# Differential attention inside a transformer block: accumulators copied out of PSUM, squares on VectorE, the causal mask as a matmul

## The chip, the cores and the metric

One Trainium2 chip, all 8 NeuronCores. Each core computes one element of a batch of 8, with no exchange between cores. The metric is the time of the slowest core in microseconds (us), from its first to its last instruction. Most executions of a kernel agree to 0.3%. Some fall into a slower state, in which cores of one die, or of both, show a lower granted TensorE clock (0.83 in place of 0.95 in the 5348.14 us execution of run 1 below); those runs are marked slow and are left out of every comparison.

## The reference, cut to what matters

A block of a hybrid encoder for 2048 frames of width 2048: one RMS norm and input projection, two mixers side by side (differential attention and an mLSTM), a gated merge, an MLP, a gated embedding, a last norm. Only the attention is touched here. It has 8 heads, each with two softmax maps of 64 channels over one value of 128:

```python
s = einsum('bqhmd,bkhmd->bhmqk', q * 64**-0.5, k)     # m = 2 maps per head
mask = (key // 64) <= (query // 64)                   # chunks of 64 frames
a = softmax(where(mask, s, NEG_INF))
w = a[:, :, 0] - lam * a[:, :, 1]
o = rmsnorm(einsum('bhqk,bhkd->bqhd', w, v), sub_g)   # over the 128 channels of a head
```

## The kernel before

Attention runs in units. A unit is a query tile of 256 rows (`qt`) against a pair of key blocks (`jp`); a head has 36 units, and tile `qt` has `qt + 1` of them, the last being the diagonal one. Scores go to PSUM banks 0 to 3 (two units in flight), the exponentials to SBUF, and the products with the values accumulate in banks 4 and 5. A 129th column of ones makes the softmax sum. Between the units, a filler issues matmuls of other jobs (the next head's K and Q, a V job, gates, the mLSTM's convolution) into banks 6 and 7. The program issues a list to each engine. ScalarE and VectorE work through theirs in order.

```python
def attn(h):
    for u in range(36 * h, 36 * h + 36):
        _, qt, jp = UN[u]
        B.act(E[u % 3], <scores of u>, AF.Exp, scale=0.125)          # ScalarE
        if jp == qt:                                                 # the causal mask
            B.memset("dve", e_[64:128, :, 0, 0:64], 0.0)
            B.memset("dve", e_[64:128, :, 1, 128:192], 0.0)
        s_mm(u + 1)                                                  # TensorE: next scores
        yield                                                        # TensorE: 3 to 4 filler matmuls
        av_mm(u)                                                     # TensorE: exponentials x values
        tick()                                                       # work that was put off
        if jp == qt:
            finalize(h, qt)
            # ... cut: after tiles 3 and 7, ya_norm two units later, ya_out six units later

def finalize(h, qt):
    for i in range(2):                                               # two blocks of 128 rows
        acc, r_ = <bank 4 + i>, rsb[b % 4]
        # VectorE: reciprocal of the two sums, r2 = r1 * -lambda   (cut)
        B.ts("dve", o_head[:, b, :], acc[:, 0, 0:128], r_[:, 0:1], ALU.mult)
        B.stt("dve", o_head[:, b, :], acc[:, 1, 0:128], r_[:, 2:3], o_head[:, b, :], ALU.mult, ALU.add)
        B.act(sqj, o_head[:, b, :], AF.Square, accum=ssa[h % 2][:, b:b + 1])   # ScalarE
```

The softmax here doesn't subtract the row's maximum and nothing guards it: scores larger than these inputs give would overflow.

Of the kernel before, what the change touches and what calls it, by code (L numbers as in the profile page):

```python
# [7 lines left out]
F32 = mybir.dt.float32  # L8
BF16 = mybir.dt.bfloat16
U8 = mybir.dt.uint8  # L10
AF = mybir.ActivationFunctionType
ALU = mybir.AluOpType
# [226 lines left out]
def build():  # L239
    B = Builder()  # L240
# [29 lines left out]
    R = lambda off, shape, dt: cv(O_R + off, shape, dt)  # L270
# [3 lines left out]
    def small(shape, dt=F32):  # L274
        n = 1
        for s_ in shape[1:]:
            n *= s_
        nb = al(n * DTS[dt])
        o = sm[0]
        sm[0] += nb  # L280
        assert sm[0] <= O_SM + SM_BYTES, sm[0]
        return cv(o, shape, dt)
# [22 lines left out]
    ssa = [small([128, 16]) for _ in range(2)]  # L305
# [3 lines left out]
    psum = es.enter_context(nc.psum_tensor("ps", [128, 4096], F32))  # L309

    def bank(i):
        return psum[:, 512 * i:512 * (i + 1)]
# [31 lines left out]
    for t_, v_, cmp_, pat, cm in ((ident_b, 0.0, ALU.not_equal, -1, 1), (ident_f, 0.0, ALU.not_equal, -1, 1),  # L344
# [3 lines left out]
            out=t_, in_=t_, pattern=[[pat, 128]], compare_op=cmp_, fill=1.0 - v_, base=0, channel_multiplier=cm),  # L348
# [77 lines left out]
    o_head = R(24704, [128, 16, 128], F32)  # L426
    ya_tok = [R(32896 + 2048 * i, [128, 8, 128], BF16) for i in range(2)]
    yast = [R(36992 + 2048 * i, [128, 1024], BF16) for i in range(2)]
    E = [R(76288 + 2048 * i, [128, 2, 2, 256], BF16) for i in range(3)]
    sqj = R(82432, [128, 128], BF16)  # L430

    xst = [R(41088 + 8192 * i, [128, 4, 512], F32) for i in range(7)]
    nsq = [R(24704 + 2048 * i, [128, 512], F32) for i in range(3)]
# [63 lines left out]
    for t in range(4):  # L497
# [7 lines left out]
        n = 0  # L505
        for _ in work():
            n += 1
            if n < 80:
                if n % 4 == 0:
                    if next(gen, None) == "ones":  # L510
                        n = 80
# [7 lines left out]
    B.memset("pool", Vb[1][:, :, :, 128:129], 1.0)  # L519


    pend = []
    side = [iter(())]

    def tick():
        next(side[0], None)
        for it in list(pend):
            it[0] -= 1
            if it[0] <= 0:
                pend.remove(it)  # L530
                it[1]()

    def attn_units():
        return [(h, qt, jp) for h in range(8) for qt in range(8) for jp in range(qt + 1)]

    UN = attn_units()

    def s_mm(u):
        h, qt, jp = UN[u]
        kv, qv = KQ[h % 2][:, 0, :], KQ[h % 2][:, 1, :]  # L540
        sb = 2 * (u % 2)
        for jj in range(2):
            j = 2 * jp + jj
            for m in range(2):
                B.mm(bank(sb + m)[:, jj * 256:(jj + 1) * 256], kv[64 * m:64 * m + 64, j * 128:(j + 1) * 128],
                     qv[64 * m:64 * m + 64, qt * 256:(qt + 1) * 256], True, True)

    def av_mm(u):
        h, qt, jp = UN[u]
        e_ = E[u % 3]  # L550
        vv = Vb[h // 4]
        last = jp == qt
        for i in range(2):
            for jj in range(2):
                if last and jj > i:
                    continue
                j = 2 * jp + jj
                for m in range(2):
                    B.mm(bank(4 + i)[:, m * 256:m * 256 + 129], e_[:, m, jj, i * 128:(i + 1) * 128], vv[:, j, h % 4, :],
                         j == 0 and m == 0, last and jj == i and m == 1, skip=True)  # L560

    def finalize(h, qt):
        for i in range(2):
            b = 2 * qt + i
            acc = bank(4 + i).rearrange("p (m d) -> p m d", m=2, d=256)
            r_ = rsb[b % 4]
            B.op("dve", lambda e, acc=acc, r_=r_: e.reciprocal(out=r_[:, 0:2], in_=acc[:, :, 128]), [acc[:, :, 128]], [r_[:, 0:2]])  # L567
            B.tt("dve", r_[:, 2:3], r_[:, 1:2], neglam, ALU.mult)
            B.ts("dve", o_head[:, b, :], acc[:, 0, 0:128], r_[:, 0:1], ALU.mult)
            B.stt("dve", o_head[:, b, :], acc[:, 1, 0:128], r_[:, 2:3], o_head[:, b, :], ALU.mult, ALU.add)  # L570
            B.act(sqj, o_head[:, b, :], AF.Square, accum=ssa[h % 2][:, b:b + 1])

    def ya_norm(h, hf):
        s8 = slice(8 * hf, 8 * hf + 8)
        ss, rs = ssa[h % 2][:, s8], rsa[h % 2][:, s8]
        B.ts("pool", rs, ss, 1.0 / 128.0, ALU.mult, EPS, ALU.add)
        B.tt("pool", rs, rs, nhalf[:, 0:8], ALU.pow)
        for b in range(8):
            B.ts("dve", ya_tok[hf][:, b, :], o_head[:, 8 * hf + b, :], rs[:, b:b + 1], ALU.mult)

    def ya_out(h, hf):
        bk = fb.get()
        for b in range(8):
            B.tp(bank_bf(bk)[:, b * 128:(b + 1) * 128], ya_tok[hf][:, b, :], ident_b)
        B.act(yast[hf], bank_bf(bk), AF.Copy, scale=subg)
        B.dma("sp", f"ya{hf}", scr_ya[h * 2 + hf], yast[hf])

    def attn(h):
        u0 = 36 * h
        for u in range(u0, u0 + 36):  # L590
            _, qt, jp = UN[u]
            if u == 0:
                s_mm(0)
            e_ = E[u % 3]
            sb = 2 * (u % 2)
            B.act(e_.rearrange("p m j q -> p (m j q)"), psum[:, 512 * sb:512 * sb + 1024], AF.Exp, scale=0.125)
            if jp == qt:
                B.memset("dve", e_[64:128, :, 0, 0:64], 0.0)
                B.memset("dve", e_[64:128, :, 1, 128:192], 0.0)
            if u + 1 < len(UN) and UN[u + 1][0] == h:  # L600
                s_mm(u + 1)
            yield
            if u + 1 < len(UN) and UN[u + 1][0] != h:
                s_mm(u + 1)
            av_mm(u)
            tick()
            if jp == qt:
                finalize(h, qt)
                if qt in (3, 7):
                    pend.append([2, lambda h=h, hf=qt // 4: ya_norm(h, hf)])  # L610
                    pend.append([6, lambda h=h, hf=qt // 4: ya_out(h, hf)])
# [264 lines left out]
    for h in range(8):  # L876
        nf = 0
        nextq = None
        if h < 7:
            nextq = kq_job(h + 1)  # L880
            fill.add(nextq)
            nf += 128
        if h == 2:
            fill.add(v_job(1))
            nf += 64
        if h == 3:
            nf += 192
        if h == 4:
            fill.add(gates())
            nf += 40  # L890
        if h == 7:
            fill.add(mqk_job(0, 0))
            nf += 128
        drive(attn(h), 36, nf)
        if h == 3:
            fill.drain()
        elif h < 7:
            fill.drain(nextq)
# [57 lines left out]
    def tmp():  # L956
        cnt["t"] += 1
        return tmps[cnt["t"] % 6]
# [44 lines left out]
    for hf in range(2):  # L1003
# [10 lines left out]
        for np_ in range(8):  # L1014
            k, w = wget(f"wo{np_}")
            for nn in range(2):
                n = 2 * np_ + nn
# [8 lines left out]
                while lagged:  # L1026
                    a_ = lagged.pop(0)
# [6 lines left out]
        for qd in range(4):  # L1034
            for np_ in range(8):
                k, w = wget(f"up{qd}_{np_}")
                for nn in range(2):
                    n = 2 * np_ + nn
                    for tt in range(2):
                        bk = mm_chain(lambda kc: w[:, kc, nn * 128:(nn + 1) * 128], lambda kc: h2[:, kc, tsl[tt]], 16)  # L1040
                        r_ = tmp()
# [9 lines left out]
            for np_ in range(8):  # L1051
                k, w = wget(f"dn{qd}_{np_}")
                for nn in range(2):
                    n = 2 * np_ + nn
                    for tt in range(2):
                        bk = mm_chain(lambda kc: w[:, kc, nn * 128:(nn + 1) * 128], lambda kc: uT[:, kc, tsl[tt]], 16)
                        q = tmp()
# [28 lines left out]
        for np_ in range(8):  # L1086
            k, w = wget(f"pg{np_}")
            for nn in range(2):
                n = 2 * np_ + nn
# [110 lines left out]
```

## Time and profile before

4874.08 us, median of 2 runs (4872.96 to 4875.2). The profile's core took 4865.1 us. How the lines are read is told with them in the prediction; the table has only the stage in question, for that core.

| attention, 860.7 us | per head |
|---|---|
| heads 0, 1, 6 (filler: the next K and Q) | 95.2, 95.6, 95.7 us |
| head 2 (and half of a V job) | 103.1 us |
| head 3 (and the other half) | 123.5 us |
| head 4 (and the gates' matmuls) | 109.0 us |
| head 5 (and the gates' recursion on VectorE) | 111.3 us |
| head 7 (the convolution's job as filler) | 127.3 us |

Heads are cut at the start of their first exponential, the stage at the start of its first and its last one.

### The profile page before, as it was taken

How to read it: one execution, taken by the hardware profiler on the slowest of the kernel's cores; microseconds unless marked ns; L12 is line 12 of the kernel's file. 1: busy time of each engine (PE TensorE's matmuls, PEld its weight loads, DVE VectorE, ACT ScalarE, POOL GpSimd, SP SyncE). 2: the span in 40 equal slices, each digit the busy share in tenths (PEclk: the TensorE clock that was granted, in tenths of full speed). 3: DMA queues.
4: the chain of work that ended last, by engine and by line, in shares of the span. 5: the costliest groups of instructions: out<-in, count | busy, mean ns of one | idle time of the engine just before them, and what ended most of it. 6: DMA issues, size and time to landing. Idle time of an engine off the chain costs nothing.

```text
span 4865.1 us, 59380 instructions; the slowest of 8 cores (4850.0 to 4865.1 us)
## 1 busy us (share of the span) xinstructions
PE 4236.3 (87%) x21472; PEld 1950.3 (40%) x21472; DVE 1568.0 (32%) x3090; ACT 1149.2 (24%) x2037; POOL 512.7 (11%) x743
## 2 busy tenths in 40 slices
PE   3778876768677678999999999999899899999986
PEld 1334443333333233444444444444344344444432
DVE  3322223233444542122222323232343232323235
ACT  2344433442333321111112010101333101010232
POOL 3200000000011010000012000000333100000122
PEclk9889978879899889999999999999999999999998
DMA  6101110001110122222255444444538444444434
GB/s 166 35 16 23 23 23 14 16 14 27 22 33 17 28 70 66 54 48 57 48 124 115 78 78 75 74 77 78 108 58 184 98 77 78 78 77 74 76 65 95
DMA packets 84319, 312.36 MB, mean 64 GB/s; under 512 B 7872, under 2 KB 31552, under 8 KB 56640
## 3 DMA queue, kind: packets, MB, share of 16 engines
q0 software_dynamic: 31504, 225.49, 25.9%
q1 hardware_dynamic: 52528, 83.07, 5.7%
q8 instruction: 177, 2.90, 0.2%
q14 instruction: 110, 0.90, 0.1%
HBM read 500.98 MB, written 33.03 MB: 110 GB/s over the span
## 4 chain that ended last, share of the span: by engine, by line
PE 74%; DVE 9%; ACT 5%; issue 5%; DMA 4%; POOL 2%; DVEq 0%; ACTq 0%; SPq 0%; POOLq 0%
PE ps L180 74%; DVE big L167 5%; ACT big L138 5%; DMA big<-xT 3%; POOL big L156 2%; DVE big L153 1%; DVE big L156 1%; DMA big<-pT 1%; PE ps L183 1%; DVEq L222 0%; DMA out<-big 0%; DVE big L567 0%; DVE big L173 0%; ACTq L222 0%; POOL big L153 0%
## 5 line engine op out<-in xcount | busy, mean ns | idle before, releaser
L180 PE MATMUL ps<-big 128*128 128x512 bf16 (+5 forms) x21084 | 4208.1, 364 | 476.3 <-ACT big L138 206.1
L180 PEld LDWEIGHTS ps<-big 128*128 128x128 bf16 (+2 forms) x21084 | 1920.7, 101 | 2742.0 <-issue 817.4
L138 ACT ACTIVATE big<-ps 128x512 f32<-128x512 f32 (+4 forms) x992 | 648.7, 663 | 2385.0 <-PE ps L180 2214.0
L156 DVE TENSOR_TENSOR big<-big 128x512 bf16<-128x512 f32 (+4 forms) x755 | 436.4, 578 | 784.6 <-ACT big L138 727.2
L138 ACT ACTIVATE big<-big 128x512 f32<-128x512 f32 (+3 forms) x722 | 415.2, 598 | 992.0 <-DVE big L167 532.8
L167 DVE SCALAR_TENSOR_TENSOR big<-big 128x512 f32<-128x512 f32 (+2 forms) x576 | 378.9, 671 | 432.5 <-ACT big L138 396.4
L156 POOL TENSOR_TENSOR big<-big 128x512 f32<-128x512 f32 (+2 forms) x369 | 370.1, 1005 | 630.1 <-ACT big L138 601.9
L156 DVE TENSOR_TENSOR big<-big,ps 128x512 f32<-128x512 f32 (+1 forms) x322 | 220.5, 685 | 609.1 <-PE ps L180 548.7
L189 POOL DMA_DIRECT2D big<-wt x214 | 116.8, 546 | 2660.8 <-PE ps L180 2643.8
L167 DVE SCALAR_TENSOR_TENSOR big<-big,ps 128x512 f32<-128x512 f32 (+1 forms) x312 | 189.4, 607 | 564.8 <-PE ps L180 497.9
L167 DVE SCALAR_TENSOR_TENSOR big<-ps,big 128x128 f32<-128x128 f32 (+1 forms) x192 | 87.4, 463 | 179.0 <-DMA big<-xT 89.0
L183 PE MATMUL ps<-big 128*128 128x128 bf16 x388 | 43.4, 260 | 116.2 <-DVE big L156 65.2
L138 ACT ACTIVATE big<-ps,big 128x256 f32<-128x256 f32 (+3 forms) x124 | 76.4, 631 | 262.2 <-POOL big L156 130.6
L173 DVE CAST big<-ps 128x512 bf16<-128x512 f32 x64 | 44.1, 690 | 197.6 <-PE ps L180 196.4
L153 POOL TENSOR_SCALAR big<-big 128x1 f32<-128x1 f32 (+1 forms) x80 | 15.2, 190 | 851.4 <-DVE big L167 518.0
L153 DVE TENSOR_SCALAR big<-ps,big 128x128 f32<-128x128 f32 (+1 forms) x192 | 75.8, 395 | 83.9 <-PE ps L180 69.2
L176 DVE MEMSET big<- 64x128 bf16 (+1 forms) x132 | 21.3, 162 | 243.0 <-ACT big L138 230.5
L153 DVE TENSOR_SCALAR big<-big 128x128 bf16<-128x128 f32 (+3 forms) x261 | 69.1, 309 | 80.7 <-ACT big L138 52.9
L183 PEld LDWEIGHTS ps<-big 128*128 128x128 bf16 x388 | 32.1, 117 | 134.9 <-issue 132.1
L567 DVE RECIPROCAL big<-ps 128x2 f32<-128x2 f32 x128 | 21.1, 165 | 72.6 <-PE ps L180 72.2
L156 DVE TENSOR_TENSOR big<-ps,big 128x128 bf16<-128x128 f32 (+1 forms) x65 | 18.4, 284 | 28.9 <-PE ps L180 28.9
L173 POOL COPY big<-big 128x3 f32<-128x3 f32 x48 | 8.9, 185 | 163.3 <-ACT big L138 163.3
(18 smaller groups left out, 84.9 us busy)
## 6 DMA issues: line engine op xcount, KB each, us to landing
big<-wt POOLq DMA_DIRECT2D x214, 1024.0 KB, 7.9
big<-xT SPq DMA_DIRECT2D x16, 1024.0 KB, 8.8
big<-xT SPq DMA_DIRECT2D x32, 512.0 KB, 7.1
out<-big SPq DMA_DIRECT2D x64, 256.0 KB, 5.7
scr_m<-big SPq DMA_DIRECT2D x60, 128.0 KB, 1.8
big<-scr_m SPq DMA_DIRECT2D x30, 256.0 KB, 6.6
scr_ya<-big SPq DMA_DIRECT2D x16, 256.0 KB, 2.0
scr_yb<-big SPq DMA_DIRECT2D x32, 128.0 KB, 1.7
```

The source lines that it names most:

```text
L138: self.op("act", lambda e: e.activation(out=out, in_=in_, func=func, **kw), rd, wr)
L153: self.op(eng, lambda e: e.tensor_scalar(out=out, in0=in0, scalar1=s1, scalar2=s2, op0=op0, **kw), rd, wr)
L156: self.op(eng, lambda e: e.tensor_tensor(out=out, in0=in0, in1=in1, op=op), [in0, in1], [out])
L167: self.op(eng, lambda e: e.scalar_tensor_tensor(out=out, in0=in0, scalar=scalar, in1=in1, op0=op0, op1=op1, **kw), rd, wr)
L173: self.op(eng, lambda e: e.tensor_copy(out=out, in_=in_), [in_], [out])
L176: self.op(eng, lambda e: e.memset(ap, val), [], [ap])
L180: self.op("pe", lambda e: e.matmul(out, lhsT=lhsT, rhs=rhs, start=start, stop=stop, **kw), [lhsT, rhs], [out])
L183: self.op("pe", lambda e: e.transpose(out=out, in_=in_, identity=ident), [in_, ident], [out])
L189: self.op(queue, lambda e: e.dma_start(out=out, in_=in_, **kw), [in_], [out], dma=sem)
L567: B.op("dve", lambda e, acc=acc, r_=r_: e.reciprocal(out=r_[:, 0:2], in_=acc[:, :, 128]), [acc[:, :, 128]], [r_[:, 0:2]])
```

## The change

Its intent is to free what the next query tile needs as soon as a tile ends. The accumulators are copied to SBUF at once and finalized from there. The squares for the head's RMS norm leave ScalarE's list for VectorE's. The mask is added to the scores inside PSUM by a small matmul (-30000 on the forbidden keys), so that nothing stands between the exponential and the matmul that uses it. As a side effect, the diagonal exponential covers 768 columns in place of 1024. Eight scalings per half head become one. In the diff, the set-up of the two mask tiles, the change of the layout of `E` and the shorter exponential are left out.

```diff
 def s_mm(u):
+    diag = jp == qt
     for jj in range(2):
+        q0 = 128 if diag and jj else 0
         for m in range(2):
-            B.mm(<256 columns>, kv[...], qv[...], True, True)
+            B.mm(<256 - q0 columns>, kv[...], qv[...], True, not diag, skip=diag)
+        if diag:
+            for m in range(2):
+                B.mm(<64 columns>, mask_k[64 * m:64 * m + 64, :], mask_q[64 * m:64 * m + 64, :], False, True, skip=True)
 def finalize(h, qt):
     for i in range(2):
+        B.copy("dve", accS[qt % 2][i], <bank 4 + i>[:, :, 0:129])
+    for i in range(2):
-        acc = <bank 4 + i>
+        a_ = accS[qt % 2][i]          # and a_ for acc in the four steps that follow
...
-        B.act(sqj, o_head[:, b, :], AF.Square, accum=ssa[h % 2][:, b:b + 1])
+        B.stt("dve", sqj, o_head[:, b, :], 1.0, o_head[:, b, :], ALU.mult, ALU.mult, accum=ssa[h % 2][:, b:b + 1])
 def ya_norm(h, hf):
-        for b in range(8):
-            B.ts("dve", ya_tok[hf][:, b, :], o_head[:, 8 * hf + b, :], rs[:, b:b + 1], ALU.mult)
+        B.tt("dve", ya_tok[hf], o_head[:, s8, :], rs.unsqueeze(2).to_broadcast([128, 8, 128]), ALU.mult)
 def attn(h):
-            if jp == qt:
-                B.memset("dve", e_[64:128, :, 0, 0:64], 0.0)
-                B.memset("dve", e_[64:128, :, 1, 128:192], 0.0)
```

More of the change, by code (lines that the diff above doesn't have):

```diff
@@ L428, in build @@
     yast = [R(36992 + 2048 * i, [128, 1024], BF16) for i in range(2)]
-    E = [R(76288 + 2048 * i, [128, 2, 2, 256], BF16) for i in range(3)]
+    E = [R(76288 + 2048 * i, [128, 2, 512], BF16) for i in range(3)]
     sqj = R(82432, [128, 128], BF16)
+    accS = [[R(82816 + 1152 * (2 * b + i), [128, 2, 129], F32) for i in range(2)] for b in range(2)]
+    mask_k = R(87424, [128, 128], BF16)
+    mask_q = R(87680, [128, 64], BF16)
     xst = [R(41088 + 8192 * i, [128, 4, 512], F32) for i in range(7)]
@@ L519, in build @@
     B.memset("pool", Vb[1][:, :, :, 128:129], 1.0)
+    B.memset("dve", mask_k, 0.0)
+    for m in range(2):
+        B.memset("dve", mask_k[64 * m:64 * m + 1, 64:128], -30000.0)
+    B.memset("dve", mask_q, 1.0)
     pend = []
@@ L541, in s_mm, with exp_s @@
         sb = 2 * (u % 2)
+        diag = jp == qt
         for jj in range(2):
             j = 2 * jp + jj
+            q0 = 128 if diag and jj else 0
             for m in range(2):
-                B.mm(bank(sb + m)[:, jj * 256:(jj + 1) * 256], kv[64 * m:64 * m + 64, j * 128:(j + 1) * 128],
-                     qv[64 * m:64 * m + 64, qt * 256:(qt + 1) * 256], True, True)
+                B.mm(bank(sb + m)[:, jj * 256:jj * 256 + 256 - q0], kv[64 * m:64 * m + 64, j * 128:(j + 1) * 128],
+                     qv[64 * m:64 * m + 64, qt * 256 + q0:(qt + 1) * 256], True, not diag, skip=diag)
+            if diag:
+                for m in range(2):
+                    B.mm(bank(sb + m)[:, jj * 256:jj * 256 + 64], mask_k[64 * m:64 * m + 64, :],
+                         mask_q[64 * m:64 * m + 64, :], False, True, skip=True)
+    def exp_s(u):
+        _, qt, jp = UN[u]
+        n = 384 if jp == qt else 512
+        sb = 2 * (u % 2)
+        B.act(E[u % 3][:, :, 0:n], psum[:, 512 * sb:512 * sb + 1024].rearrange("p (m q) -> p m q", m=2, q=512)[:, :, 0:n],
+              AF.Exp, scale=0.125)
     def av_mm(u):
@@ L557, in av_mm @@
                 j = 2 * jp + jj
+                q0 = 256 if last and jj else jj * 256 + i * 128
                 for m in range(2):
-                    B.mm(bank(4 + i)[:, m * 256:m * 256 + 129], e_[:, m, jj, i * 128:(i + 1) * 128], vv[:, j, h % 4, :],
+                    B.mm(bank(4 + i)[:, m * 256:m * 256 + 129], e_[:, m, q0:q0 + 128], vv[:, j, h % 4, :],
                          j == 0 and m == 0, last and jj == i and m == 1, skip=True)
@@ L563, in finalize @@
         for i in range(2):
+            B.copy("dve", accS[qt % 2][i], bank(4 + i).rearrange("p (m d) -> p m d", m=2, d=256)[:, :, 0:129])
+        for i in range(2):
             b = 2 * qt + i
-            acc = bank(4 + i).rearrange("p (m d) -> p m d", m=2, d=256)
+            a_ = accS[qt % 2][i]
             r_ = rsb[b % 4]
-            B.op("dve", lambda e, acc=acc, r_=r_: e.reciprocal(out=r_[:, 0:2], in_=acc[:, :, 128]), [acc[:, :, 128]], [r_[:, 0:2]])
+            B.op("dve", lambda e, a_=a_, r_=r_: e.reciprocal(out=r_[:, 0:2], in_=a_[:, :, 128]), [a_[:, :, 128]], [r_[:, 0:2]])
             B.tt("dve", r_[:, 2:3], r_[:, 1:2], neglam, ALU.mult)
-            B.ts("dve", o_head[:, b, :], acc[:, 0, 0:128], r_[:, 0:1], ALU.mult)
-            B.stt("dve", o_head[:, b, :], acc[:, 1, 0:128], r_[:, 2:3], o_head[:, b, :], ALU.mult, ALU.add)
-            B.act(sqj, o_head[:, b, :], AF.Square, accum=ssa[h % 2][:, b:b + 1])
+            B.ts("dve", o_head[:, b, :], a_[:, 0, 0:128], r_[:, 0:1], ALU.mult)
+            B.stt("dve", o_head[:, b, :], a_[:, 1, 0:128], r_[:, 2:3], o_head[:, b, :], ALU.mult, ALU.add)
+            B.stt("dve", sqj, o_head[:, b, :], 1.0, o_head[:, b, :], ALU.mult, ALU.mult, accum=ssa[h % 2][:, b:b + 1])
     def ya_norm(h, hf):
@@ L593, in attn @@
                 s_mm(0)
-            e_ = E[u % 3]
-            sb = 2 * (u % 2)
-            B.act(e_.rearrange("p m j q -> p (m j q)"), psum[:, 512 * sb:512 * sb + 1024], AF.Exp, scale=0.125)
-            if jp == qt:
-                B.memset("dve", e_[64:128, :, 0, 0:64], 0.0)
-                B.memset("dve", e_[64:128, :, 1, 128:192], 0.0)
+            exp_s(u)
             if u + 1 < len(UN) and UN[u + 1][0] == h:
```

## The prediction

> **What bounds the kernel now.** I read the list of cores first: all eight lie between 4850.0 and 4865.1 us at clock 0.94, so no die is disturbed. Then I cut the slowest core's run into its stages. The view of windows gives, per stretch, each engine's busy time and the granted TensorE clock (PEclk).
>
> ```profile
> core 1: us, PE busy (x) PEld busy (x) DVE busy (x) ACT busy (x) POOL busy (x), PEclk, DMA share, GB/s
> 0.00:196.20 196.20, 103.67 (x397) 40.67 (x397) 72.07 (x102) 53.36 (x90) 72.11 (x65) 0.94 0.44 114
> 196.20:1056.90 860.70, 644.25 (x4966) 324.84 (x4967) 234.49 (x878) 370.57 (x599) 35.10 (x49) 0.85 0.10 19
> ```
>
> The second stretch is attention, the only stage that the change touches: 860.7 us for 8 heads. No engine is full there: TensorE 75% busy, ScalarE 43%, VectorE 27%, DMA 10%. TensorE's waits in that stretch:
>
> ```profile
> PE ps L180 <- ACT big L138: 172.7, 66, 11.1
> PE ps L180 <- DVE big L176: 29.7, 11, 4.4
> PE ps L180 <- DVE big L173: 12.7, 12, 2.1
> ```
>
> So 202.4 us of idle TensorE end with an exponential or with the mask's memset, in 77 waits for 64 query tiles: about one per tile. The timeline of one such place (the end of a query tile in head 1) shows why:
>
> ```profile
> 364.56 3.00 PE L180 MATMUL ps<-big 64*128 64x256 bf16 x22
> ...
> 366.14 0.17 DVE L567 RECIPROCAL big<-ps 128x2 f32<-128x2 f32 x1
> ...
> 367.58 0.31 ACT L138 ACTIVATE big<-big 128x128 bf16<-128x128 f32 x1 [2.99 <-DVE big L567]
> ...
> 368.39 0.35 DVE L167 SCALAR_TENSOR_TENSOR big<-ps,big 128x128 f32<-128x128 f32 x1
> 368.89 0.31 ACT L138 ACTIVATE big<-big 128x128 bf16<-128x128 f32 x1 [0.91 <-DVE big L167]
> 369.11 0.19 ACT L138 ACTIVATION_READ_ACCUMULATOR big<-big 128x1 f32 x1
> 369.20 1.92 ACT L138 ACTIVATE big<-ps 128x1024 bf16<-128x1024 f32 x2
> 370.61 1.45 PE L180 MATMUL ps<-big 128*128 128x129 bf16 x13 [3.05 <-ACT big L138]
> ```
>
> The next unit's exponential has its scores ready, but stands behind the two squares in ScalarE's queue, and these wait for VectorE's finalizing chain. ScalarE idles 2.99 + 0.91 us, TensorE 3.05 us. The stall is paid twice, as the windows around it show:
>
> ```profile
> 358.00:367.40 9.40, 9.40 (x85) 4.90 (x84) 2.13 (x8) 4.10 (x4) 0.00 (x0) 1.00 0.00 0
> 367.40:370.60 3.20, 0.16 (x1) 0.02 (x1) 1.03 (x5) 2.11 (x6) 0.00 (x0) 1.00 0.00 0
> 370.60:375.00 4.40, 4.39 (x29) 2.19 (x30) 0.00 (x0) 2.07 (x3) 0.00 (x0) 0.61 0.02 4
> 375.00:384.00 9.00, 9.00 (x87) 5.02 (x85) 1.05 (x4) 4.59 (x5) 0.00 (x0) 1.00 0.00 0
> ```
>
> At full clock 172 matmuls took 18.4 us, 107 ns each; the 29 after the stall took 4.4 us (152 ns) at clock 0.61. 29 x 45 ns = 1.3 us more. Attention's mean of 0.85 is this, head after head.
>
> [...]
>
> **The change, part by part.**
> *Squares to VectorE.* This takes 128 ACTIVATEs (309 ns) and 128 accumulator reads (187 ns) from ScalarE, 63 us that bind nothing, and with them every wait of the exponential for VectorE. The next exponential then starts as its scores are there, under the last matmuls of the tile. That is the whole gain.
> *Copies out of PSUM.* Two per tile at about 0.42 us. Banks 4 and 5 are free about 0.45 and 0.9 us after the last matmul, where before it was after the chain of 2.6 us (366.14 to 368.74). TensorE comes back to them after the next scores and the filler, about 1.2 us (366.2 to 367.4). So they just fit; without the copies the finalizing chain would be the new wait.
> *Finalizing from SBUF.* VectorE's chain per 128-row block: reciprocal 0.16, product 0.16, scale about 0.28 (the 128x128 SBUF row), combine about 0.35, square about 0.35, accumulator read about 0.1, five handovers of 0.1: 1.9 us. With copies 0.8 + 2 x 1.9 = 4.6 us per tile, against 2.6. Times 64 is 294 us for 166; the memsets save 21. VectorE goes to about 340 of some 670 us: not a bound on average.
> *The mask.* It removes two memsets between exponential and matmul (0.5 us of latency). It adds 4 matmuls of 64 columns and halves two of 256, net about 0.1 us per tile, 6 us. Diagonal exponentials shrink by a quarter, from 1.02 to about 0.8 us, off the path.
> *One normalization for eight.* 8 x 0.2 us become about 1.1 us, off the path.
>
> Now TensorE's time for each head, once it does not wait. Head 1 has 562 matmuls: 562 x 107 ns = 60 us (it takes 95.6). Heads 0, 6 likewise, 5 and 7 about 60 to 62. Head 2 has 64 more 512-column ones at 0.215: 74. Head 3 has 187 more: 100. Head 4 has 256 small ones for the gates, about 0.06 each: 75. Sum 552 us.
> To this I add per head: masks 0.8; the wait for the last K/Q copy (L173 above) 1.5; and a backlog of VectorE at the start of a head, where tiles of 1, 2 and 3 units of 1.66 us follow one another while each brings 4.6 us of finalizing. The copies of the first tile wait for the previous head's chain (about 2.4 us), those of the second about 1.2: 3.6 us; and the cold clock after it 1.7. That is 7.6 x 8 = 61.
> Head 5 runs the gate recursion on VectorE (31 tiny operations in 8 us), which holds the copies up: 12. Head 7 fills with the convolution job: each of 8 evacuations holds ScalarE for about 4.8 us (copy, scale, a wait for three VectorE steps, Tanh), TensorE has about 1.6 us to cover it with an exponential of 1 us to come: 4.3 us of stall and 1.6 of cold clock each, 47. The change leaves that wait in place.
> 552 + 61 + 12 + 47 = 672 us for 860.7: 189 less. 4874 - 189 = 4685 us. Check from the other side: of the 202 us idle some 45 stay in heads 5 and 7 and some 25 come back at head starts, 130 gained; TensorE's 644 busy us shrink as the clock goes from 0.85 to about 0.94, by about 60. Sum 190.
>
> **Rivals.** (a) *VectorE becomes the wait.* Its chain grows by 75%, and its first-come queue also holds the K/Q copies and, in head 7, the convolution. Against it: four of five later tiles come 5 us or more apart. If each tile still lost 1.2 us plus some cold clock, 64 x 1.8 = 115 us would come back: about 4790, inside 2%. (b) *The exponentials become the bound.* 36 x 1.02 = 37 us per head against 60 of TensorE; in the warm stretch each had 0.7 to 1.1 us to spare. Speaks against. (c) *The clock recovers wholly and backlog is hidden by filler.* Then heads fall to 62 and the time to about 4640. (d) *A later stage gives it back.* Weight tiles might come too late for faster heads; DMA share 0.10 at 19 GB/s speaks against. What follows attention depends on data, not on the time of day.
>
> **Range and chances.** The gain from the squares is seen directly in 202 us of waits; what is uncertain is what returns through VectorE (20 to 90 us) and the clock (20 to 70 us). I predict 4685 us, 4635 to 4750 for 8 in 10. Faster by over 2% needs 97 us less, half of the estimate: 0.95. Within 2%: 0.045. Slower: 0.005.
>
> **What would show it.** Right: attention near 670 us at clock about 0.94; no wait of ScalarE for the reciprocal's line; TensorE's wait on exponentials down from 173 to about 50, most of it in head 7; new waits on PSUM copies, in the first units of heads; TensorE's other stages unchanged to a few us. Wrong: waits on copies at nearly every tile (rival a), a clock still near 0.85, or attention over 760 us.

## The result, and the profile after

4677.31 us, median of 2 runs (4676.12 to 4678.49), 197 us less. The ratio to before is 0.9588, with a 95% interval of 0.9554 to 0.9622. All ratios here are the mean time of one kernel's fast runs over that of the other's in the same rounds, so they are not quite the ratio of the medians quoted. In a later set the same kernel came out at 0.9583.

The windows of the changed kernel's slowest core, in the columns shown before; the second line is attention:

```profile
0.00:197.30 197.30, 103.97 (x394) 40.83 (x401) 72.32 (x106) 53.26 (x90) 72.32 (x65) 0.94 0.45 113
197.30:861.70 664.40, 563.18 (x5129) 311.80 (x5219) 276.72 (x1025) 316.71 (x346) 35.18 (x49) 0.94 0.13 25
861.70:4677.40 3815.70, 3471.59 (x15788) 1584.42 (x16108) 1262.45 (x2107) 724.47 (x1346) 407.02 (x630) 0.96 0.37 72
```

Attention went from 860.7 to 664.4 us, 196.3 less, which is the whole change. The first stretch took 196.2 before and 197.3 now. What comes after took 3808.2 (4865.1 - 1056.9) and takes 3815.7 here, on a different core; in the second profile of the changed kernel attention took 662.0 and the rest 3807.7. Nothing was given back later.

The 196.3 us have two parts that the windows give directly. TensorE's idle time is the length less its busy time: 216.5 us before, 101.2 now. Its busy time went from 644.25 to 563.18, though it has 252 instructions more (5219 by the weight loads, whose records are complete, against 4967). One correction is needed: the trace of the changed kernel lacks 90 of its matmul records (5129 for 5219 weight loads; that of before lacks one), and 61 short gaps, 11.2 us, stand where they are missing ("issue" in the list below; run 9, whose records lack one, has one such gap). So some 126 us of idle time and some 70 us of busy time went. The busy time fell as the granted clock rose from 0.85 to 0.94. In the clock records, 44 stretches at half clock (a recorded 0.5), 252.6 us in all, became 13 with 85.3 us. Not all of the 44 are the work of stalls: the longest, in head 4 (34.1 us from 702.65), went on while the trace has TensorE busy for 28.0 us of it, with 202 of the gates' narrow matmuls.

TensorE's waits in attention, after:

```profile
PE ps L180 <- DVE big L173: 48.2, 31, 5.9
PE ps L180 <- ACT big L138: 34.0, 21, 5.1
PE ps L180 <- issue: 11.2, 61, 0.9
```

Waits for exponentials fell from 172.7 to 34.0 us, and 22.9 of these lie in head 7. The 29.7 us on the mask's memset are gone. New are the waits on L173, the line of VectorE's copies: 48.2 us, against 12.7 before. With 3.1 us more of the same kind at the transposes (L183), they are of two forms: 28.7 us on the new copies of the accumulators (128x258), 22.6 us on the older copies that empty the filler's banks (128x512). The "issue" line is the missing records.

The end of a query tile in head 1, the same (seventh) tile as the one shown of before:

```profile
314.06 4.33 PE L180 MATMUL ps<-big 128*128 128x512 bf16 x35
314.56 0.69 DVE L173 CAST big<-ps 128x512 bf16<-128x512 f32 x1 [6.19 <-PE ps L180]
314.57 1.02 ACT L138 ACTIVATE big<-ps 128x1024 bf16<-128x1024 f32 x1 [1.01 <-PE ps L180]
315.32 0.76 DVE L173 COPY big<-ps 128x258 f32<-128x258 f32 x2
315.93 1.02 ACT L138 ACTIVATE big<-ps 128x1024 bf16<-128x1024 f32 x1 [0.34 <-PE ps L180]
```

TensorE runs through without a break. The exponential starts 0.34 us after the one before it, waiting for its scores alone. The two copies take 0.76 us and are over before the accumulators are wanted again; the rest of the chain runs on beside the next units.

At the start of a head that does not hold. The last tile of head 0 and the first of head 1:

```profile
259.02 0.76 DVE L173 COPY big<-ps 128x258 f32<-128x258 f32 x2 [6.20 <-PE ps L180]
259.69 0.15 DVE L590 RECIPROCAL big<-big 128x2 f32<-128x2 f32 x1
...
262.93 0.08 DVE L167 DVE_READ_ACCUMULATOR big<-big 128x1 f32 x1
262.93 0.69 DVE L173 CAST big<-ps 128x512 bf16<-128x512 f32 x1
263.54 0.75 DVE L173 COPY big<-ps 128x258 f32<-128x258 f32 x2
264.10 0.72 PE L180 MATMUL ps<-big 128*128 128x129 bf16 x8 [2.02 <-DVE big L173]
```

The copies of head 1's first tile (263.54) stand behind the finalizing of head 0's last tile and behind a filler copy. TensorE waits 2.02 us for them. Of the 28.7 us of waits on such copies, 21.3 lie after the first three tiles of a head, and heads 5 and 7 have 18.6.

### The profile page after: what moved, and what is told of

It is laid out like the page before. It is cut to its first block, busy times and chain, and to the rows that moved or that the text cites. A ratio compares the mean times of both kernels' runs of the same rounds, so it can differ in the third digit from the quotient of the medians.

```text
span 4677.4 us, 59243 instructions; the slowest of 8 cores (4665.8 to 4677.4 us)
## 1 busy us (share of the span) xinstructions
PE 4138.8 (88%) x21311; PEld 1937.1 (41%) x21728; DVE 1611.5 (34%) x3238; ACT 1094.4 (23%) x1781; POOL 514.5 (11%) x743
## 4 chain that ended last, share of the span: by engine, by line
PE 76%; DVE 8%; issue 5%; DMA 4%; ACT 4%; POOL 2%; another core or an unknown queue 0%; DVEq 0%; ACTq 0%; SPq 0%; POOLq 0%
PE ps L180 76%; DVE big L167 5%; ACT big L138 4%; DMA big<-xT 3%; POOL big L156 2%; DVE big L153 1%; DVE big L156 1%; DMA big<-pT 1%; DVE big L173 1%; PE ps L183 0%; DVEq L222 0%; DMA out<-big 0%; POOL big L153 0%; DVE big L817 0%
## 5 line engine op out<-in xcount | busy, mean ns | idle before, releaser
L180 PE MATMUL ps<-big 128*128 128x512 bf16 (+5 forms) x20923 | 4112.8, 357 | 389.1 <-DVE big L156 141.7
L138 ACT ACTIVATE big<-ps 128x512 f32<-128x512 f32 (+5 forms) x992 | 640.2, 651 | 2485.1 <-PE ps L180 2239.7
L156 DVE TENSOR_TENSOR big<-big 128x512 bf16<-128x512 f32 (+5 forms) x771 | 456.0, 592 | 804.2 <-ACT big L138 729.1
L167 DVE SCALAR_TENSOR_TENSOR big<-big 128x512 f32<-128x512 f32 (+3 forms) x832 | 461.4, 564 | 445.0 <-ACT big L138 386.5
L138 ACT ACTIVATE big<-big 128x512 f32<-128x512 f32 (+3 forms) x594 | 375.5, 661 | 757.5 <-DVE big L167 489.3
L167 DVE SCALAR_TENSOR_TENSOR big<-big,ps 128x512 f32<-128x512 f32 (+1 forms) x312 | 189.4, 607 | 563.7 <-PE ps L180 464.2
L183 PE MATMUL ps<-big 128*128 128x128 bf16 x388 | 39.5, 246 | 120.5 <-DVE big L156 74.8
L173 DVE COPY big<-ps 128x258 f32<-128x258 f32 (+1 forms) x140 | 53.3, 417 | 153.6 <-PE ps L180 148.5
L153 DVE TENSOR_SCALAR big<-big 128x128 f32<-128x128 f32 (+3 forms) x261 | 79.3, 311 | 71.5 <-ACT big L138 51.3
L167 DVE SCALAR_TENSOR_TENSOR big<-ps,big 128x512 f32<-128x512 f32 x64 | 42.4, 688 | 174.3 <-DMA big<-xT 99.6
L173 DVE CAST big<-ps 128x512 bf16<-128x512 f32 x64 | 44.1, 689 | 136.0 <-PE ps L180 136.0
L183 PEld LDWEIGHTS ps<-big 128*128 128x128 bf16 x388 | 28.9, 110 | 139.0 <-issue 137.1
L153 DVE TENSOR_SCALAR big<-ps,big 128x256 bf16<-128x256 f32 x64 | 30.9, 483 | 69.0 <-PE ps L180 65.5
L173 POOL COPY big<-big 128x3 f32<-128x3 f32 x48 | 9.0, 187 | 137.5 <-ACT big L138 115.7
L590 DVE RECIPROCAL big<-big 128x2 f32<-128x2 f32 x128 | 20.4, 159 | 0.2
```

Source lines behind the costliest of these rows:

```text
L138: self.op("act", lambda e: e.activation(out=out, in_=in_, func=func, **kw), rd, wr)
L153: self.op(eng, lambda e: e.tensor_scalar(out=out, in0=in0, scalar1=s1, scalar2=s2, op0=op0, **kw), rd, wr)
L156: self.op(eng, lambda e: e.tensor_tensor(out=out, in0=in0, in1=in1, op=op), [in0, in1], [out])
L167: self.op(eng, lambda e: e.scalar_tensor_tensor(out=out, in0=in0, scalar=scalar, in1=in1, op0=op0, op1=op1, **kw), rd, wr)
L173: self.op(eng, lambda e: e.tensor_copy(out=out, in_=in_), [in_], [out])
L180: self.op("pe", lambda e: e.matmul(out, lhsT=lhsT, rhs=rhs, start=start, stop=stop, **kw), [lhsT, rhs], [out])
```

## The experiments

Every kernel gave the reference's result. Theory A is the prediction's: the exponential waits because of where the squares stand in ScalarE's list; the copies are needed so that the accumulator banks do not become the next wait; the clock adds its own share. The rivals are named with each run. Medians are of the fast runs.

**1. The squares alone.** The kernel before, with this edit:

```diff
-            B.act(sqj, o_head[:, b, :], AF.Square, accum=ssa[h % 2][:, b:b + 1])
+            B.stt("dve", sqj, o_head[:, b, :], 1.0, o_head[:, b, :], ALU.mult, ALU.mult, accum=ssa[h % 2][:, b:b + 1])
```

> The kernel before, with the squares on VectorE and nothing else changed: accumulators are still finalized from PSUM, the mask is still two memsets. Theory of the prediction: the exponentials no longer wait for VectorE, but the accumulator banks come free only at the end of the longer finalizing chain, about 3.05 us after the last matmul, of which 1.2 us are covered; TensorE then waits 1.6 to 1.9 us per query tile for the combine step instead of 3.05 us for the exponential. Time about 4750 us (4715 to 4795), with waits of TensorE on VectorE's PSUM-reading combine of some 100 us. Rival (the squares' move is the whole change, the copies are decoration): about 4680 us.

Five of six runs fell into the slow state, which leaves one, 4754.49 us. So it was run again:

> The squares alone on VectorE, again, because only one of the six runs of the first time was undisturbed (4754 us). Theory as before: 4750 us (4735 to 4765), between the kernel before and the changed one, as the finalizing chain still holds the accumulator banks. Rival (squares are the whole gain): 4680 us.

Four fast runs of seven: 4747.62, 4752.56, 4792.04 and 4809.67; ratio 0.9793 (0.9704 to 0.9882). In the last two, the slowest cores of one die were already 40 to 70 us behind the other die. The 4792 run was profiled: its cores 0 to 3 show a mean clock of 0.945 to 0.946, its cores 4 to 7 one of 0.953 to 0.956. So the two lower ones and the 4754 of the first set are the better figure: about 4752, some 120 us less than before. TensorE's waits in its attention stage, on an undisturbed core:

```profile
PE ps L180 <- DVE big L167: 71.9, 57, 8.3
PE ps L180 <- DVE big L176: 31.1, 14, 5.6
PE ps L180 <- ACT big L138: 22.4, 15, 4.0
```

The wait for exponentials fell from 172.7 to 22.4 us, and in 57 places stands a wait for L167, the combine step that reads the accumulators in PSUM. One wait has taken the place of another, a shorter one: 71.9 us, where I had said about 100. Theory A holds and the rival (4680 us) falls.

**2. The copies alone.** The kernel before with the copies and the finalizing from SBUF, squares still on ScalarE.

```diff
+            B.copy("dve", accS[qt % 2][i], <bank 4 + i>[:, :, 0:129])     # and a_ for acc below
```

> The kernel before, with the copies out of PSUM and finalizing from SBUF, the squares still on ScalarE in their old place. Theory of the prediction: the squares wait for a chain that is longer by the copies, about 3.2 us against 2.6, and the exponential behind them too: slower by about 0.6 us per tile, 4910 us (4880 to 4940). Rival (the PSUM banks were the real wait, the trace blames the exponential because it came last): clearly faster than before, 4800 us or less.

4929.9 us, ratio 1.0112 (1.0088 to 1.0136): slower by 1.1%. TensorE waits longer for the same thing:

```profile
PE ps L180 <- ACT big L138: 199.0, 66, 11.8
PE ps L180 <- DVE big L176: 35.4, 15, 4.6
```

That is 199.0 us for 172.7, and 58 stretches at half clock for 44. Releasing the banks is worth nothing while the exponential is held elsewhere; the longer chain in front of the squares is paid in full. The rival falls. The same copies that cost 55 us here are worth about 50 once the squares are away (run 1 against run 4, which also has the single normalization; that was never tried alone), so the value of one part can't be read off with the other missing.

**3. The mask alone.** The kernel before with the mask by matmuls.

> The kernel before, with the causal mask by matmuls and nothing else changed. Theory of the prediction: 0.5 us of latency goes only where a diagonal exponential stands directly before its matmuls, two or three places per head: about 10 us less, 6 us more for the added matmuls; 4870 us (4855 to 4880). Rival (the memsets between exponential and matmul carry a good part of the gain, as 29.7 us of TensorE's idle time ended with them): 4845 us or less.

4860.4 us, ratio 0.9992 (0.9924 to 1.0061); one of its four fast runs, 4911, has two cores that lag. The other three lie at 4854 to 4862, some 15 us under before, at the low end of the expected range and above the rival's 4845; the interval of the ratio by itself would allow up to 37 us. The waits say why it gains so little: those on the memset (29.7 us) are gone and those on the exponential rose from 172.7 to 199.9.

```profile
PE ps L180 <- ACT big L138: 199.9, 74, 9.6
```

The memset only came last in a wait that would have ended just before it.

**4. Everything but the mask.** The changed kernel with memsets again.

```diff
+        if jp == qt:
+            B.memset("dve", e_[64:128, :, 0:64], 0.0)
+            B.memset("dve", e_[64:128, :, 384:448], 0.0)
```

> The changed kernel with the mask by memsets again (full score matmuls, full exponentials, two memsets per tile on VectorE). Theory: at the start of a head, where VectorE is behind, the memsets stand behind the previous tile's finalizing and hold the matmuls: some 1.5 us at about three tiles per head, 36 us, less 6 us for the mask matmuls saved: about 4705 us (4685 to 4730). Rival (the mask by matmul is worth nothing beyond its own 6 us): 4671 us within 10.

4700.1 us, ratio 0.9655 (0.9634 to 0.9676). Beside the changed kernel (0.9588 and 0.9583 in the other sets) that is 0.7% or some 33 us. TensorE's longest waits:

```profile
PE ps L180 <- DVE big L176: 40.0, 21, 5.6
PE ps L180 <- DVE big L173: 31.2, 16, 7.2
```

With VectorE now in charge of all finalizing, a memset in its list stands behind the chain of the previous tile: 40.0 us in 21 places. So the mask, worth some 15 us by itself, is worth about 33 beside the other two parts (the shorter diagonal exponential is in both figures).

**5. Stall kept, clock kept up.** The kernel before, with the score matmuls ahead of each stall issued 12 times, same values into the same bank:

```diff
-                s_mm(u + 1)
+                for _ in range(12 if u and UN[u - 1][1] == UN[u - 1][2] else 1):
+                    s_mm(u + 1)
```

> The kernel before, with the score matmuls that stand in front of each stall issued 12 times over (same values into the same bank, about 2.6 us of matmuls), so that TensorE works through most of the wait while the chain that it waits for stays as it is. Theory of the prediction: the stall costs twice, by itself and by the lower clock after it (1.3 us each by the one place read); the repeats take away the second part: 56 to 63 places by about 1.3 us, 4800 us (4775 to 4830), granted clock in attention from 0.85 to over 0.93. Rival (the clock follows load but costs nothing on a path that waits anyway): 4874 us within 15, or slower by what the repeats overrun.

4830.2 us, ratio 0.9907 (0.9890 to 0.9925): some 2770 useless matmuls more, and 45 us less, at the far end of the expected range. Its attention stage:

```profile
197.20:1015.80 818.60, 709.50 (x7629) 436.65 (x7739) 234.87 (x878) 370.91 (x599) 35.10 (x49) 0.95 0.11 20
```

It took 818.6 us for 860.7, at clock 0.95; 10 stretches at half clock in place of 44. The rival (the clock costs nothing) falls. My size was wrong: I had 1.3 us at each of some 60 places, 74 us. With 34 stretches fewer, the 42 us of the stage are 1.24 us each; a stall did not always bring a slow stretch. In the trace of before, 44 of the 66 gaps of over 1.5 us have one that begins during the gap or within 1.6 us of its end, 7 fell into one that was running, 15 brought none. Whether the clock's part of the whole change is these 42 us or up to the 70 by which TensorE's busy time fell stays open: here the chain of the next stall may eat some of what the faster matmuls gain, and the repeats may overrun in places.

**6. The squares on ScalarE after all, but late.** The changed kernel with the squares issued two units after the tile's end:

```diff
-            B.stt("dve", sqj, o_head[:, b, :], 1.0, o_head[:, b, :], ALU.mult, ALU.mult, accum=...)
+                pend.append([2, lambda h=h, qt=qt: squares(h, qt)])     # AF.Square on ScalarE
-                    pend.append([2, lambda ...: ya_norm(h, hf)])
+                    pend.append([3, lambda ...: ya_norm(h, hf)])
```

> The changed kernel with the squares back on ScalarE, but issued two units after the tile's end, behind exponentials that are due earlier. Theory (place in the queue matters, not the engine; VectorE's backlog makes the remaining waits on copies): no waits of the exponentials return; VectorE's chain per tile falls from 4.0 to about 3.2 us and TensorE's waits on VectorE copies fall from 48 us to about 33; 4655 us (4640 to 4670). Rival (any square on ScalarE delays the exponentials): slower than 4690 us.

4665.4 us, ratio 0.9584 (0.9567 to 0.9601): against the changed kernel's 0.9588 and 0.9583 no difference that these rounds resolve, so the 20 us that I expected did not come. What the run does show is that the rival is wrong: 126 squares back on ScalarE cost nothing when they are issued behind the exponentials that are due. It is the place in the list, not the engine, that made the stall of before. In the trace, waits on copies fell from 48.2 to 40.7 us, and those on exponentials, of which I had expected none to return, rose from 34.0 to 40.3:

```profile
PE ps L180 <- DVE big L173: 40.7, 26, 7.5
PE ps L180 <- ACT big L138: 40.3, 34, 5.9
```

The attention stage of this profile took 651.5 us (664.4 and 662.0 in the two of the changed kernel), a gain of 10 us or so that the times of the whole kernel can't confirm.

**7. More work on VectorE.** The changed kernel with every square done twice, 0.8 us more per tile.

> The changed kernel with each square on VectorE done twice, 0.8 us more per tile (51 us of VectorE work). Theory: only the first tiles of a head and the ones beside other VectorE work feel it: 3 or 4 tiles of 8 by 0.8 us, with some clock: 4700 us (4688 to 4712). Rival (a) of the prediction (VectorE sets the pace of every tile): 64 x 0.8 = 51 us or more, 4728 us and up. Rival (it is all hidden): 4677 us.

4694.2 us, ratio 0.9644 (0.9623 to 0.9665), some 27 to 30 us more than the changed kernel. The work added is 128 x 0.4 = 51 us; about half of it shows. The waits on copies went from 48.2 to 60.2 us:

```profile
PE ps L180 <- DVE big L173: 60.2, 30, 7.2
```

So VectorE's chain sets TensorE's pace in part of the tiles, as the prediction had it, and neither in all (the rival's 4728) nor in none (4677).

**8. The convolution's Tanh put off.** Run 6, and in the convolution job that fills head 7 the last two steps issued seven matmuls into the next chain:

```diff
+        def rest():
             B.act(cth, ac, AF.Tanh, scale=16.0 if kind == 0 else 1.0)
             B.stt("dve", dst[...], cth, 1.0, ac, ALU.add, ALU.mult)
+        return rest
...
+                    if q == 7 and rest:
+                        rest.pop()()
```

> The late squares of the run before, and the convolution's last two steps (Tanh on ScalarE and the product on VectorE) issued seven matmuls into the next chain, so that ScalarE's queue does not stand still while VectorE does its three steps. Theory: what is left of TensorE's waits on exponentials (34 us, nearly all in head 7) goes for the greater part, with the lower clock there: 25 to 40 us out of head 7; the same job also fills the mLSTM stage, where the same queue stands still: perhaps 20 us more. 4600 us (4570 to 4640). Rival (the convolution is bound by VectorE's own work): 4645 us or more.

4635.9 us, ratio 0.9522 (0.9507 to 0.9537), 30 us less than run 6 on the same chip. Head 7, and the mLSTM's stage that follows it, in this kernel (here the boundary lies 5 us after the last exponential's start, in both kernels):

```profile
748.00:831.80 83.80, 62.75 (x580) 33.63 (x588) 45.43 (x122) 57.08 (x94) 6.17 (x14) 0.98 0.12 22
831.80:1640.00 808.20, 588.28 (x2708) 274.70 (x2763) 355.74 (x805) 245.85 (x566) 78.71 (x266) 0.87 0.16 32
```

and the same stretch of run 6:

```profile
741.80:852.60 110.80, 74.31 (x590) 38.83 (x587) 45.62 (x120) 57.78 (x94) 6.16 (x14) 0.85 0.08 16
```

Head 7 fell from 110.8 to 83.8 us (105.8 to 78.8 by the usual cut) with hardly a change in any other engine's work; the clock there rose from 0.85 to 0.98. TensorE's waits for exponentials in head 7 fell from 25.0 to 8.5 us: for the greater part they were ScalarE's list standing still for VectorE. The further 20 us that I thought possible in the mLSTM stage did not come (808.2 us, about the 809 of before and after). Range met, reason half met. This is the fastest kernel within what the rounds resolve.

**9. The same work in another order.** The changed kernel with the finalizing of block 0 issued one unit later and that of block 1 two units later, so that copies should not stand behind a whole chain. (The normalization moves from two units later to three.)

```diff
-        for i in range(2):                       # in finalize, after the copies
+                for i in range(2):               # in attn, after finalize
+                    pend.append([1 + i, lambda h=h, qt=qt, i=i: block(h, qt, i)])
```

> The changed kernel with the same work in another order: the two copies still stand at the tile's end, but the finalizing steps of its first block are issued one unit later and those of the second two units later, so that a following tile's copies, or a filler bank's copy, stand behind at most one block (1.6 us) and not behind the whole chain. Theory (the remaining waits on copies come from the order in VectorE's queue, not from the amount of its work): waits on accumulator copies from 28.7 us to about 12, on filler copies from 22.6 to about 15, with some clock: 4655 us (4640 to 4668). Rival (VectorE has too much work at the start of a head): within 6 us of 4677.

4682.5 us, ratio 0.9611 (0.9595 to 0.9626), against 0.9583 (0.9566 to 0.9600) for the changed kernel in the same rounds: slower by 0.3%, if by anything. My theory failed as I had put it. The waits on copies are 49.9 us, as before, but not in the same places: those on the filler's copies halved, from 22.6 to 11.3 us, and those on the accumulators' rose from 28.7 to 38.6. The first tile's copies in each head hardly hold TensorE any more (2.02 us became 0.39 in head 1), and the second tile's do, in five more heads like this one. VectorE, ahead of the second tile's copies in head 1:

```profile
266.53 0.76 DVE L167 SCALAR_TENSOR_TENSOR big<-big 128x128 f32<-128x128 f32 x2
267.21 0.08 DVE L167 DVE_READ_ACCUMULATOR big<-big 128x1 f32 x1
268.06 1.22 DVE L156 TENSOR_TENSOR big<-big 128x1024 bf16<-128x1024 f32 x1 [0.77 <-POOL big L156]
...
270.81 0.76 DVE L173 COPY big<-ps 128x258 f32<-128x258 f32 x2
271.38 0.48 PE L180 MATMUL ps<-big 128*128 128x129 bf16 x3 [4.04 <-DVE big L173]
```

The product of the normalization has come to stand in front of the copies, waits 0.77 us there for GpSimd's power and takes 1.22, and a block stands behind it. The rival, that VectorE simply has too much to do in the first units of a head, fits: apart from that 0.77 us it has hardly a pause from the copies at the head's start (260.45) to this one. But the new order also brought in a wait of its own, so the run does not decide cleanly between order and amount. Runs 6 and 7, which change the amount and move the waits on copies with it (40.7, 48.2, 60.2 us), show that the amount counts; where the waits went in this run shows that the order does too.

**10. That order on top of run 8.**

> The order of the run before, on top of the late squares and the lagged Tanh (4636 us): 15 us less by the same reasoning, 4620 us (4608 to 4630). Rival: late squares had already taken what the order can give, 4636 us within 6.

4637.2 us, ratio 0.9523 (0.9505 to 0.9542), no different from run 8's 0.9522. The rival was right about the time. In the traces the order did take waits on copies away (26.9 us for run 8's 38.8), but waits on exponentials rose (28.8 for 23.8) and the clock in attention was 0.96 for 0.98.

**11. The changed kernel again,** for the comparisons above.

> The changed kernel itself once more, on the same chip as the three runs above, for comparison: 4677 us within 8.

4667.3 us, 0.9583 (0.9566 to 0.9600), 10 us under the first set's median and a little outside the expected width; before measured 4865.6 to 4876.3 beside it.

The parts together, as ratios to before:

| | ratio |
|---|---|
| mask alone | 0.9992 |
| copies alone | 1.0112 |
| squares alone | 0.9793 (undisturbed runs about 0.976) |
| squares, copies, one normalization | 0.9655 |
| all (the change) | 0.9588, 0.9583 |
| and late squares, put-off Tanh | 0.9522 |

## Why the prediction was right

It said 4685 us and 4677.3 was measured. Point by point:

- *What holds TensorE.* Right, and shown by runs 1, 2 and 6: the exponential behind the blocked squares. Run 6 is the sharpest, since it puts the squares back on ScalarE and the stall does not return. The sign that the prediction named is there too: ScalarE waited 190.5 us for the reciprocal's line before, and that wait is gone from its list.
- *The copies just fit, and without them the chain would be the new wait.* Right: 421 ns each where 0.42 us was foreseen (an estimate from the nearest copy in the trace of before, 64x256 out of PSUM at 739.10, 417 ns), no break at the tile's end that is shown, and run 1 shows that new wait at 57 places. It holds for most tiles, not all: 18 waits on the copies remain, 28.7 us.
- *VectorE's chain, 4.6 us per tile.* Too long: it measured 4.0 us (315.32 to 319.31 at the tile shown). The square took 293 ns for my 350, and the two copies overlap to 0.76. My estimates of the other steps were close: scale 288 ns for 280, combine 352 for 350, read-out of the accumulator 84 for 100, and the one normalization for eight 1223 for 1100. Its total in the stage was 277 us, not 340; besides the shorter steps, the 340 had counted the handovers between them as busy.
- *Masks cost 6 us net and remove latency.* For the mask alone this is about right (10 less and 6 more expected, some 15 less in the undisturbed runs). The 6 was an estimate; the trace of after has 18.2 us of TensorE's busy time for the 252 mask matmuls, 72 ns each. The diagonal exponentials took 810 ns where 0.8 us was foreseen. That in the changed kernel memsets would queue behind the chain, and the mask so be worth 33 us, was not in the prediction; I wrote it as the expectation of run 4 only after seeing the result.
- *Per head.* Here the total hides errors that cancel. (Two unit times behind the predicted row: 0.215 us for a matmul of 512 columns is the pace later in the trace of before, 7560 matmuls in 1633.90 us; 0.06 us for a matmul of the gates was an estimate, and the trace of after has 256 of them in 7.9 us of busy time, 31 ns each.)

| head | 0 | 1 | 2 | 3 | 4 | 5 | 6 | 7 | sum |
|---|---|---|---|---|---|---|---|---|---|
| predicted | 67.6 | 67.6 | 81.6 | 107.6 | 82.6 | 80.6 | 67.6 | 116.6 | 672 |
| measured | 61.5 | 69.4 | 88.1 | 104.4 | 78.5 | 86.9 | 69.3 | 106.3 | 664 |

  Head 0 has no head before it, so no backlog: my 7.6 us applied to 8 heads where 7 have it. Heads 2 and 5 have 6 us more than I gave them, from a wait that I missed: the filler's own banks are emptied by VectorE, and that copy stands behind the chain as well (22.6 us in all, 7.1 in head 2 with up to 3.78 at a time, 7.5 in head 5). Head 7 I took too high by 10 us, with each of 8 evacuations stalling TensorE 4.3 us, 34 us in all; waits for exponentials there came to 22.9.
- *Idle time 130 us less, busy time 60 us less.* Measured: some 126 and 70, with the missing records allowed for. The clock was predicted at 0.94 and came out at 0.94. The clock by itself, tested in run 5, gave 45 us for the 74 expected of that run; that was mis-sized because I took one place for typical.
- *Rivals.* (a), VectorE as the pace of every tile, fell by run 7; in part of the tiles it is so. (b), the exponentials as the bound, fell: attention takes 629 us in run 8 with the same exponentials. (c), full recovery, did not come: run 8 has (c)'s time by another way, with the put-off Tanh, and its heads 1 and 6 still take 69.3 and 69.1 us, not 62. (d), a later stage giving it back, fell: the rest took 3807.7 us for 3808.2.
- *Two slips.* Rival (a)'s sum is 4685 + 115 = 4800, not 4790 (still inside 2%). And TensorE's last matmul in the timeline ends at 367.56, so the time that covers the copies was 1.4 us, not 1.2. Neither changes the argument.

## What to carry to other kernels

When an engine's list is worked through in order, look at what stands in front of the instruction that the critical engine waits for, and whether that thing is itself waiting for a third engine: issuing it two units later can be as good as moving it to another engine (run 6: 0.9584, beside 0.9588 and 0.9583). Try the parts of a change both alone and with one left out, as here the copies were a loss of 55 us alone and a gain of about 50 once the squares were away. And count a stall of TensorE higher than its length, since a slow stretch of some microseconds may go with it (here at 44 of the 66 gaps of over 1.5 us; 43 of the 44 stretches of that stage lasted 3.4 to 10.2 us).

## What the traces show of the clock and of short steps

- Gaps of 3.05 us (before) and 2.02 us (after, head 1) were followed within 1 us by a stretch of 3.4 us at half clock. Of the 30 gaps of 2.8 to 3.5 us in the attention stage of before, 24 have a stretch at half clock beginning in the gap or within 1.6 us of its end, and 6 have none. So the length of the gap alone does not tell whether a slow stretch comes.
- In the profiles of before and after the last 3000 us, dense matmuls on 8 cores, ran at 0.98 on every core, with only full and half clock in the records. In the profiles of two disturbed runs of the squares alone, one die shows a lower mean clock than the other: 0.938 to 0.942 on cores 4 to 7 against 0.951 to 0.953 in the first set, 0.945 to 0.946 on cores 0 to 3 against 0.953 to 0.956 in the second. So the lower clock belongs to some executions and not to all: five of six runs of that kernel came out in the slower state, up to 12% longer (5348.14 us against 4754.49) with the clock of one die down to 0.83. What lowers it was not shown; the slowest runs were not profiled.
- A copy of 258 fp32 from PSUM took VectorE 421 ns, and two in a row took 0.76 us. Reading out an accumulator took 84 ns on VectorE (after) and 187 ns on ScalarE (before).
